# Closing a stage token tile by token tile, with the last rows of the first columns and all rows of the second columns together

## The chip, the cores and the metric

The kernel runs on one core of one Trainium2 chip. The metric is the device time of one execution in microseconds (us); the median of three runs of the kernel before is 2530.16 us.

## The reference

The input is x, 512 tokens by 1024 features, in fp32. It goes through two blocks. The first has two layers: a state-space mixer (S5, with a gated output) and a multi-head latent attention (MLA), each followed by a squared-ReLU feed-forward. The second has two layers of a sparse attention with a spatial gate (DSA), each followed by a gated feed-forward (SwiGLU) with a per-layer embedding p. After each of these eight steps the result is added to the scaled input of the step and normalised:

```python
h = layer_norm(DN_ALPHA * h + mix, ln_mix_g[layer], ln_mix_b[layer])
h = layer_norm(DN_ALPHA * h + sq_relu_mlp(h, w_ff1[layer], w_ff2[layer]), ln_ffn_g[layer], ln_ffn_b[layer])
...
x = layer_norm_2(ALPHA * x + mix, ln1_g[i], ln1_b[i])
...
x = layer_norm_2(ALPHA * x + ffn + ple, ln2_g[i], ln2_b[i])
```

So every step ends with a product of an activation (512 tokens by some rows) with a weight of 1024 columns, the residual sum and a layer norm over the 1024 columns. These eight ends are called closings 1 to 8 here: 1 is the S5 output, 3 MLA, 5 and 7 DSA (`proj_ln`); 2 and 4 are the squared-ReLU feed-forwards, 6 and 8 the SwiGLU ones (`plain`). Closing 8 writes the output.

## The kernel before, in words

**Products.** An fp32 product is three matmuls (`mm3`, L262 to L267): each operand is split into a high and a low part, and high by high, high by low and low by high are summed in PSUM. Rows of a weight are taken in groups of 128, called kts here. A weight arrives by DMA as `wr` (two buffers, four kts of 512 columns in one); `wpiece` (L245) makes pieces of two kts from it: ACT casts the high part `wh`, and VectorE or GpSimd subtracts it to get the low part `wl` (five buffers of each). GpSimd takes the next pieces while the counter `lo_pool` is above zero (L252); it is set to `LP` = 10 at L320, and inside MLA and DSA GpSimd is the engine for all of them.

**A closing.** The 512 tokens are four tiles of 128, the 1024 columns two halves of 512. A pass of eight kts over one tile and one half is 24 matmuls into one PSUM bank. Before the change the first half runs piece by piece over all four tiles, and its four banks are then added to the residual (`update`, L402). The second half has its four pieces ready first and runs tile by tile (`tm_gen` with `stagger`, L323 to L332). After each tile `close` (L422) normalises it on VectorE: residual update from PSUM, statistics (L360, L361), the first pair of full-width operations (L119, one for each half), an inverse square root of 1-element operations (L114, L116, L109), and the second pair (L119). The two x tiles that come out are turned by 8 TensorE transposes (L127) into the feature-major operand of the next stage, cast by ACT (`xh`) and split by VectorE (`xl`). These transposes are queued as pending and are issued one tile at a time: here when more than two are pending (L331), the rest in the next stage's first matmuls (`fm_start`, L462). In MLA and DSA the first half of the closing fills in among the attention's own steps (`proj_first`, L1143).

**Order.** The tile framework's scheduler writes a fixed list of instructions for each engine; on the chip each engine takes its list in order and waits at its head. An instruction that is not ready so holds all behind it on that engine.

Of the kernel before, what the change touches and what calls it, by code (L numbers as in the profile page):

```python
# [8 lines left out]
F32R = mybir.dt.float32r  # L9
# [7 lines left out]
P = 128  # L17
SEQ = 512
NT = SEQ // P
# [28 lines left out]
LP = 10  # L48
# [7 lines left out]
class Cols:  # L56


    def __init__(self, *halves):
        self.halves = halves  # L60
# [6 lines left out]
class Net:  # L67
    def __init__(self, tc, ctx):
        self.tc = tc
        self.nc = tc.nc  # L70
        self.ctx = ctx
        self.n = 0
        self.pending = []
        self.lo_eng = tc.nc.vector
        self.ple = None
        self.lo_pool = 0

    def name(self, tag):
        self.n += 1
        return f"{tag}{self.n}"  # L80
# [161 lines left out]
            self.nc.sync.dma_start(raw[sl] if sl is not None else raw, src)  # L242
        return raw

    def wpiece(self, src):  # L245
        a, b = src.shape[1:]
        hi = self.tile(self.wp, [P, a, b], F32R, "wh", 5)
        lo = self.tile(self.wp, [P, a, b], F32R, "wl", 5)
        self.nc.scalar.copy(hi, src)  # L249
        eng = self.lo_eng  # L250
        if self.lo_pool:
            self.lo_pool -= 1  # L252
            eng = self.nc.gpsimd
        self.tt(lo, src, hi.bitcast(F32), OP.subtract, eng)
        return hi, lo
# [773 lines left out]

    def plain(self, pool, n, H, w, row, gb, final):  # L1030

        gb = self.gb(*gb)
        if final is None:
            self.fm_ln()
        parts = []
        for k in range(2):
            for t in range(2):
                hl = self.tile(pool, [P, 2, n, 256], F32R, "wq", 4)
                self.split(hl[:, 0], hl[:, 1], H[k][t])
                parts.append(hl)  # L1040
        pick = lambda i: (lambda k: Cols(*(parts[k // n * 2 + t][:, i, k % n] for t in range(2))))
        for nh in range(2):
            ev = self.close_ln(gb, nh, False, final) if nh else self.residual(False)(nh)
            self.tm(self.wslab(w, nh * 512, 512, row), list(range(2 * n)), 512, pick(0), pick(1), ev, stagger=nh == 1)

    def strassen(self, pool, n, H, w, row):

# [79 lines left out]
        put(X, 1, 0, OP.add)  # L1127
        yield

    def proj_ln(self, wsrc, xh, xl, gb, order=tuple(range(8)), first=None):  # L1130
        gb = self.gb(*gb)
        if first is None:
            self.new_r()
        self.fm_ln()
        for nh in range(2):
            ev = self.close_ln(gb, nh, True) if nh else self.residual(True)(nh)
            if nh == 0 and first is not None:
                for _ in first:
                    pass
                continue  # L1140
            self.tm(wsrc(nh), list(order), 512, xh, xl, ev, stagger=nh == 1)

    def proj_first(self, wsrc, xh, xl, order=tuple(range(8)), fine=False):  # L1143
        self.new_r()

        def evac(t, ps):
            if self.X is None:
                self.unspill()
            self.residual(True)(0)(t, ps)
        return self.tm_gen(wsrc(0), list(order), 512, xh, xl, evac, fine=fine)  # L1150


    def rope(self, dst, src, half, t, c0):
        nc = self.nc
# [98 lines left out]
    def mla_(self, pool, kv_w_a, kv_norm_g, kv_w_b, q_w_a, q_norm_g, q_w_b, w_o, gb):  # L1253
# [144 lines left out]
        oh, ol = self.fm_x()  # L1398
# [5 lines left out]
            units += [unit(head, qt, shared) for qt in range(NT)]  # L1404
        wsrc = lambda nh: self.wslab(w_o[0], nh * 512, 512)
        pick = lambda x: (lambda k: x[:, k])
        first = self.proj_first(wsrc, pick(oh), pick(ol))
        self.attend(units, 2, [(len(units), first)])
        return lambda: self.proj_ln(wsrc, pick(oh), pick(ol), gb, first=first)


    def sgu_prep(self, sgu_w, sgu_b):
# [42 lines left out]
    def dsa_(self, pool, w_in, w_o, gb, sgu_w, sgu_b, sgu_g, sgu_bt):  # L1455
# [3 lines left out]
        def wsrc(nh):  # L1459
            def src(g):  # L1460
                c = slice(nh * 512, nh * 512 + 512)
                if g[0] >= 4:
                    return [(None, w_o[g[0] * P:(g[-1] + 1) * P, c].rearrange("(k p) m -> p k m", p=P))]
                return [(slice(h * 64, h * 64 + 64), w_o[h * 256:h * 256 + 256, c].rearrange("(k p) m -> p k m", p=64))
                        for h in range(2)]
            return src
# [34 lines left out]
        with self.phase("idx") as sub:  # L1501
# [19 lines left out]
            for t in range(1, NT):  # L1521
                n = (t + 1) * P
                s = score[t]
                qs = slice(t * P, n)
                for h in range(4):
                    bk = self.bank()
                    sl = slice(h % 2 * 64, h % 2 * 64 + 64)
# [21 lines left out]
        with self.phase("sgu") as sub:  # L1549
# [3 lines left out]
            wt, bs, finish = self.sgu_prep(sgu_w, sgu_b)  # L1553
# [95 lines left out]
                        units += [unit(f, g, 2 * half + i, shared) for i in range(2)]  # L1649
            pick = lambda x: (lambda k: A[x][:, k])  # L1650
            order = list(range(4, 8)) + list(range(4))
            first = self.proj_first(wsrc, pick("h"), pick("l"), order, True)

            def some(gen, n):
                for _ in range(n):
# [4 lines left out]
                                     (len(units) + 2, first)])  # L1660


        return lambda: self.proj_ln(wsrc, pick("h"), pick("l"), gb, order, first=first)

    def swiglu(self, p, w_in, w_out, w_ple, w_pg, gb, final):
        ple, self.ple = self.ple, None
# [119 lines left out]
```

## Time and profile before

| what | value |
|---|---|
| median of 3 runs | 2530.16 us (2527.28 to 2530.75) |
| profiled execution: its time, its span | 2529.88 us, 2528.1 us |
| mean granted TensorE clock | 0.973 |
| busy: TensorE matmul, VectorE, ACT, GpSimd | 95%, 62%, 38%, 15% |
| TensorE waits of transposes for a normalised x tile | 30.8 us in 10 waits |
| from TensorE's last matmul to the span's end | 12.8 us |

TensorE is busy nearly all the time, so the shares alone say little: what can be won or lost lies in the few places where its list stands still. A transpose that waits for x (line L127 waiting for VectorE's L119) is such a place, and it stands at each closing.

### The profile page before, as it was taken

What the parts mean: (1) busy time and instruction counts of PE and PEld (TensorE: products, weight loads), DVE (VectorE), ACT (ScalarE), POOL (GpSimd) and SP (SyncE); (2) the same over time, 40 slices, a digit from 0 to 9 for tenths busy, and PEclk for the clock granted to TensorE, in tenths of its full rate; (3) what the DMA queues carried; (4) which work ended last, traced back from release to release, by engine and by line L of the source; (5) the groups of instructions that cost most, each with busy time, mean ns of one, the idle gap of its engine ahead of it and who ended that gap; (6) DMA issues with size and microseconds to landing.
All of it is one profiled execution on the core that took longest, in us unless ns stands there. A gap on an engine that the chain in (4) does not pass through costs nothing.

```text
span 2528.1 us, 30717 instructions
## 1 busy us (share of the span) xinstructions
PE 2411.3 (95%) x11961; PEld 1988.5 (79%) x11961; DVE 1559.1 (62%) x2898; ACT 968.8 (38%) x1563; POOL 389.0 (15%) x378
## 2 busy tenths in 40 slices
PE   7799999999989999999999999999989998999997
PEld 6667888888877888888776878888877687888886
DVE  8744366765666567765695573555569556355655
ACT  4213235445245335444246432333324643223331
POOL 1100110000231220000246220000034622000001
PEclk9779999999999999999999999999999999999999
DMA  4224243322221533222232235232123123423211
GB/s 110 57 57 133 84 150 101 98 88 81 85 71 51 167 92 109 92 92 67 78 127 51 84 121 179 67 133 67 60 86 127 51 86 107 167 67 117 84 59 59
DMA packets 182897, 237.55 MB, mean 94 GB/s; under 512 B 19728, under 2 KB 118816, under 8 KB 182688
## 3 DMA queue, kind: packets, MB, share of 16 engines
q1 hardware_dynamic: 182752, 235.59, 29.5%
q8 instruction: 94, 1.54, 0.3%
q14 instruction: 51, 0.42, 0.1%
HBM read 224.56 MB, written 11.01 MB: 93 GB/s over the span
## 4 chain that ended last, share of the span: by engine, by line
PE 82%; DVE 15%; ACT 2%; DMA 1%; issue 1%; SPq 0%; DVEq 0%; POOL 0%; ACTq 0%
PE ps L265 26%; PE ps L266 25%; PE ps L267 25%; PE ps L127 3%; DVE x L119 2%; PE ps L791 2%; DVE sc L1451 2%; DVE m L1450 2%; DVE x L109 1%; PE ps L789 1%; PE ps L459 1%; DVE vy L109 1%; DVE xl L109 1%; DVE ab L109 1%; DVE sc L119 1%
## 5 line engine op out<-in xcount | busy, mean ns | idle before, releaser
L109 POOL TENSOR_TENSOR wl<-wr,wh 128x1024 fp32r<-128x1024 f32 (+4 forms) x124 | 278.2, 2253 | 1810.9 <-ACT wh L249 1127.0
L249 ACT CAST wh<-wr 128x1024 fp32r<-128x1024 f32 (+4 forms) x300 | 305.7, 1021 | 578.8 <-PE ps L266 287.4
L267 PE MATMUL ps<-xh,wl 128*128 128x512 f32 x1248 | 485.9, 390 | 4.3 <-DVE wl L109 4.3
L265 PE MATMUL ps<-xh,wh 128*128 128x512 f32 x1248 | 486.2, 390 | 0.0
L266 PE MATMUL ps<-xl,wh 128*128 128x512 f32 x1248 | 486.2, 390 | 0.0
L109 DVE TENSOR_TENSOR wl<-wr,wh 128x1024 fp32r<-128x1024 f32 x176 | 217.2, 1236 | 226.5 <-ACT wh L249 225.4
L109 DVE TENSOR_TENSOR wl<-wq,wh 128x1024 fp32r<-128x1024 f32 x140 | 170.5, 1221 | 178.1 <-ACT wh L249 177.7
L267 PEld LDWEIGHTS ps<-xh,wl 128*128 128x128 f32 x1248 | 234.7, 188 | 53.4 <-DVE wl L109 4.7
L265 PE MATMUL ps<-wh,xh 128*128 128x512 f32 (+4 forms) x704 | 270.9, 386 | 4.5 <-DVE rp L109 2.0
L266 PEld LDWEIGHTS ps<-xl,wh 128*128 128x128 f32 x1248 | 234.8, 188 | 48.8
L265 PEld LDWEIGHTS ps<-xh,wh 128*128 128x128 f32 x1248 | 234.6, 188 | 48.6
L266 PE MATMUL ps<-wl,xh 128*128 128x512 f32 (+4 forms) x704 | 263.6, 375 | 0.0
L267 PE MATMUL ps<-wh,xl 128*128 128x512 f32 (+4 forms) x704 | 262.6, 376 | 0.5 <-DVE xl L109 0.5
L249 ACT CAST wh<-wq 128x1024 fp32r<-128x1024 f32 x140 | 147.3, 1052 | 284.1 <-PE ps L266 234.5
L266 PE MATMUL ps<-wl,sh 128*128 128x512 f32 x560 | 217.8, 389 | 0.0
L267 PE MATMUL ps<-wh,sl 128*128 128x512 f32 x560 | 217.5, 389 | 0.0
L265 PE MATMUL ps<-wh,sh 128*128 128x512 f32 x560 | 216.9, 389 | 0.0
L265 PEld LDWEIGHTS ps<-wh,xh 128*128 128x128 f32 x704 | 136.9, 195 | 31.4 <-ACT xh L122 3.5
L267 PEld LDWEIGHTS ps<-wh,xl 128*128 128x128 f32 x704 | 136.1, 194 | 22.1 <-DVE xl L109 1.1
L266 PEld LDWEIGHTS ps<-wl,xh 128*128 128x128 f32 x704 | 137.0, 195 | 18.5
L109 DVE TENSOR_TENSOR x<-x,ps 128x512 f32<-128x512 f32 x156 | 103.0, 681 | 73.4 <-PE ps L267 73.1
L127 PE MATMUL ps<-ident,x 128*128 128x128 f32 x576 | 97.6, 289 | 47.3 <-DVE x L119 30.8
(368 smaller groups left out, 3910.8 us busy)
## 6 DMA issues: line engine op xcount, KB each, us to landing
wr<-in_w_ffn_in_dram SPq DMA_DIRECT2D x44, 1024.0 KB, 5.1
wr<-in_w_ff_dram SPq DMA_DIRECT2D x40, 1024.0 KB, 5.5
wq<-in_w_ff_dram SPq DMA_DIRECT2D x24, 1024.0 KB, 5.1
wq<-in_w_ffn_out_dram SPq DMA_DIRECT2D x16, 1024.0 KB, 8.2
wr<-in_w_in_dram SPq DMA_DIRECT2D x12, 1024.0 KB, 5.5
wr<-in_w_ple_gate_dram SPq DMA_DIRECT2D x8, 1024.0 KB, 5.1
wr<-in_ssm_w_glu_dram SPq DMA_DIRECT2D x6, 1024.0 KB, 5.6
xs<-x SPq DMA_DIRECT2D x24, 256.0 KB, 2.0
```

The lines of the kernel that those rows point to most:

```text
L109: (eng or self.nc.vector).tensor_tensor(out, a, b, op)
L119: (eng or self.nc.vector).scalar_tensor_tensor(out, a, s, b, op0, op1)
L127: self.nc.tensor.transpose(out, in_, self.ident[:k, :k])
L249: self.nc.scalar.copy(hi, src)
L265: mm(ps, lh, rh, start=first, stop=False)
L266: mm(ps, lh, rl, start=False, stop=False)
L267: mm(ps, ll, rh, start=False, stop=last)
L459: self.nc.tensor.matmul(bk[:, c], w[:, kt], self.Xh(kt)[:, c], start=kt == 0 and w is hi, stop=False)
L789: nc.tensor.matmul(o, u[:, q * 8 + j, sl], T[:, m * 2 + h, jj], start=True, stop=False)
L791: nc.tensor.matmul(o, H[sl, r, j], ca[sl, r, j].rearrange("p d c -> p (d c)"), start=False, stop=r == 1)
L1450: self.nc.vector.max(m8, s)
L1451: self.nc.vector.match_replace(s, m8, s, -3e38)
```

## The change

A closing is cut in two functions. `begin` runs the first half of the columns with all but the last four kts, piece by piece over all tiles (in MLA and DSA as the filler among the attention's steps). `finish` has six pieces ready: the two of the last four kts of the first half (`p0`) and the four (three in closing 6, where a stage has six kts) of the second half (`p1`). For each tile it runs `p0`, the update of the first half, `p1` and the close, so a tile has 36 matmuls (30 in closings 6 and 8) where it had 24 (18). The last piece of `p1` lies in additional buffers (`sh`, `sl`). Pending transposes are issued when more than one is pending. `lo_pool` = 10 is set ahead of the six pieces, so four are left for the next stage's pieces where six were. The parameters of the norm and the residual read back from memory are loaded ahead of `finish`.

```diff
@@ -242,10 +243,13 @@
-    def wpiece(self, src):
+    def wpiece(self, src, spare=None):
         a, b = src.shape[1:]
-        hi = self.tile(self.wp, [P, a, b], F32R, "wh", 5)
-        lo = self.tile(self.wp, [P, a, b], F32R, "wl", 5)
+        if spare is None:
+            hi = self.tile(self.wp, [P, a, b], F32R, "wh", 5)
+            lo = self.tile(self.wp, [P, a, b], F32R, "wl", 5)
+        else:
+            hi, lo = (self.tile(spare, [P, a, b], F32R, tag, spare is not self.tail and 2 or 1) for tag in ("sh", "sl"))
...
@@ -1029,9 +1033,6 @@
     def plain(self, pool, n, H, w, row, gb, final):
-        gb = self.gb(*gb)
-        if final is None:
-            self.fm_ln()
...
-        for nh in range(2):
-            ev = self.close_ln(gb, nh, False, final) if nh else self.residual(False)(nh)
-            self.tm(self.wslab(w, nh * 512, 512, row), list(range(2 * n)), 512, pick(0), pick(1), ev, stagger=nh == 1)
+        wsrc = lambda nh: self.wslab(w, nh * 512, 512, row)
+        order, acc = list(range(2 * n)), []
+        for _ in self.begin(wsrc, pick(0), pick(1), order, acc):
+            pass
+        self.finish(wsrc, pick(0), pick(1), order, gb, acc, final, pool)
...
+    def pieces(self, wsrc, kts, spare=None):
+        for i in range(0, len(kts), 4):
+            g = kts[i:i + 4]
+            raw = self.wraw(wsrc(g), len(g), 512)
+            for j in range(0, len(g), 2):
+                m = min(2, len(g) - j)
+                yield self.wpiece(raw[:, j:j + m], spare if i + j + m == len(kts) else None), g[j:j + m]
+
+    def times(self, bank, t, piece, ks, xh, xl, first, last):
...
+    def begin(self, wsrc, xh, xl, order, acc):
+        m = len(order) - 4
+        for pc, ks in self.pieces(wsrc(0), order[:m]):
+            for t in range(NT):
+                if len(acc) <= t:
+                    acc.append(self.bank())
+                self.times(acc[t], t, pc, ks, xh, xl, ks[0] == order[0], False)
+                yield
+
+    def finish(self, wsrc, xh, xl, order, gb, acc, final=None, spare=None):
+        m = len(order) - 4
         gb = self.gb(*gb)
+        if final is None:
+            self.fm_ln()
+        ev0, ev1 = self.residual(False)(0), self.close_ln(gb, 1, False, final)
+        self.lo_pool = LP
+        p0 = list(self.pieces(wsrc(0), order[m:]))
+        p1 = list(self.pieces(wsrc(1), order, spare))
+        for t in range(NT):
+            for pc, ks in p0:
+                self.times(acc[t], t, pc, ks, xh, xl, False, ks[-1] == order[-1])
+            ev0(t, acc[t])
+            bk = self.bank()
+            for pc, ks in p1:
+                self.times(bk, t, pc, ks, xh, xl, ks[0] == order[0], ks[-1] == order[-1])
+            ev1(t, bk)
+            if len(self.pending) > 1:
+                self.flush()
+
+    def proj_ln(self, wsrc, xh, xl, gb, order=tuple(range(8)), first=None, acc=None):
+        order = list(order)
         if first is None:
             self.new_r()
-        self.fm_ln()
-        for nh in range(2):
-            ev = self.close_ln(gb, nh, True) if nh else self.residual(True)(nh)
-            if nh == 0 and first is not None:
-                for _ in first:
-                    pass
-                continue
-            self.tm(wsrc(nh), list(order), 512, xh, xl, ev, stagger=nh == 1)
...
+            acc = []
+            first = self.begin(wsrc, xh, xl, order, acc)
+        for _ in first:
+            pass
+        if self.X is None:
+            self.unspill()
+        with self.phase("tail") as pool:
+            self.tail = pool
+            self.finish(wsrc, xh, xl, order, gb, acc, spare=pool)
+
+    def proj_first(self, wsrc, xh, xl, order=tuple(range(8))):
         self.new_r()
...
+        acc = []
+        return self.begin(wsrc, xh, xl, list(order), acc), acc
```

In closings 1, 2 and 4 TensorE's list follows that order for tiles 0 and 1, then has the first columns of tiles 2 and 3, the transposes of tile 0, the second columns of tile 2, the transposes of tile 1, the second columns of tile 3, and the transposes of tile 2. The place that differs most is closing 5 (the same in 7): the DSA output. TensorE before, from the last matmuls of tile 2's second columns (`ps_12085`); x_11944 and x_11945 are tile 0, `ps_12149` is tile 3's second columns, x_11946 and x_11947 tile 1:

```order
L266 MATMUL ps_12085<-wl_11982,xh_11411 128x512
L267 MATMUL ps_12085<-wh_11981,xl_11412 128x512
L127 MATMUL ps_12135<-ident_68,x_11944 128x128 x4
L127 MATMUL ps_12142<-ident_68,x_11945 128x128 x4
L265 MATMUL ps_12149<-wh_11966,xh_11411 128x512
```

TensorE in the change at the same closing, from the last matmuls of tile 0's (`ps_11957`) and tile 1's (`ps_12020`) second columns; x_11883 and x_11884 are tile 0, `ps_12097` is tile 2's second columns:

```order
L270 MATMUL ps_11957<-sl_11941,xh_11419 128x512
L271 MATMUL ps_11957<-sh_11940,xl_11420 128x512
L270 MATMUL ps_12020<-sl_11941,xh_11419 128x512
L271 MATMUL ps_12020<-sh_11940,xl_11420 128x512
L269 MATMUL ps_12020<-sh_11940,xh_11419 128x512
L270 MATMUL ps_12020<-sl_11941,xh_11419 128x512
L271 MATMUL ps_12020<-sh_11940,xl_11420 128x512
L128 MATMUL ps_12070<-ident_68,x_11883 128x128 x4
L128 MATMUL ps_12077<-ident_68,x_11884 128x128 x4
L269 MATMUL ps_12097<-wh_11925,xh_11419 128x512
```

Tile 0's transposes stood behind tile 2's 24 matmuls; now they stand ahead of them, five matmuls after tile 0's own last one. (Line numbers are one to four higher in the change.)

VectorE in the change at closing 1, from the end of tile 2's inverse square root to its last pair; x_1760 and x_1762 are tile 2, x_1764 and x_1766 tile 3, `ps_2522` is tile 3's second columns, `wl_2842` a piece of the next stage's weights:

```order
L117 TENSOR_SCALAR rq_2481<-rt_2480 128x1
L110 TENSOR_TENSOR wl_2842<-wr_2839,wh_2841 128x1024
L117 TENSOR_SCALAR rq_2481<-rq_2481,rt_2480 128x1
L120 SCALAR_TENSOR_TENSOR x_1766<-x_1766,ps_2522 128x512
L110 TENSOR_TENSOR vy_2477<-vy_2477,rq_2481 128x1
L364 BN_STATS st_2549<-x_1766 128x6
L120 SCALAR_TENSOR_TENSOR x_1760<-x_1760,vy_2477,x_2256 128x512
L120 SCALAR_TENSOR_TENSOR x_1762<-x_1762,vy_2477,x_2258 128x512
```

VectorE before at closing 1, around tile 1's last pair (x_1756 and x_1758), for which the transposes wait there; `ps_2505` is tile 3's second columns:

```order
L109 TENSOR_TENSOR vy_2423<-vy_2423,rq_2427 128x1
L116 TENSOR_SCALAR vy_2473<-rs_2475 128x1
L119 SCALAR_TENSOR_TENSOR x_1756<-x_1756,vy_2423,x_2191 128x512
L119 SCALAR_TENSOR_TENSOR x_1758<-x_1758,vy_2423,x_2193 128x512
L116 TENSOR_SCALAR rt_2476<-vy_2473,ve_2472 128x1
L119 SCALAR_TENSOR_TENSOR x_1766<-x_1766,ps_2505 128x512
```

Before, the pair for which TensorE waits stood ahead of tile 3's update; in the change the pair of tile 2, whose transposes come ahead of the next stage, stands behind tile 3's update, its statistics and a piece of the next stage's weights.

## Rows read from the trace of the kernel before

**Rows 1.** The page: busy us (share of the span) and instructions of each engine.

```profile
PE 2411.3 (95%) x11961; PEld 1988.5 (79%) x11961; DVE 1559.1 (62%) x2898; ACT 968.8 (38%) x1563; POOL 389.0 (15%) x378
```

**Rows 2.** Waits of TensorE: what for, us in total, times, longest.

```profile
PE ps L127 <- DVE x L119: 30.8, 10, 5.5
```

**Rows 3.** Timeline, PE, closings 1 to 7: start, duration, work, [idle before <-releaser].

```profile
333.63 1.97 PE L127 MATMUL ps<-ident,x 128*128 128x128 f32 x8 [5.47 <-DVE x L119]
...
676.42 1.97 PE L127 MATMUL ps<-ident,x 128*128 128x128 f32 x8 [3.15 <-DVE x L119]
...
897.52 1.11 PE L127 MATMUL ps<-ident,x 128*128 128x128 f32 x4 [2.10 <-DVE x L119]
...
1240.35 1.32 PE L127 MATMUL ps<-ident,x 128*128 128x128 f32 x8 [3.21 <-DVE x L119]
...
1470.35 1.77 PE L127 MATMUL ps<-ident,x 128*128 128x128 f32 x8 [4.71 <-DVE x L119]
...
1864.56 1.32 PE L127 MATMUL ps<-ident,x 128*128 128x128 f32 x8 [1.44 <-DVE x L119]
...
1872.34 1.40 PE L127 MATMUL ps<-ident,x 128*128 128x128 f32 x8 [2.35 <-DVE x L119]
...
2101.98 1.85 PE L127 MATMUL ps<-ident,x 128*128 128x128 f32 x8 [4.71 <-DVE x L119]
...
2106.91 1.54 PE L127 MATMUL ps<-ident,a 128*128 128x128 f32 x6 [2.65 <-DMA a<-in_p_dram]
```

**Rows 4.** Timeline, DVE, closing 1: one tile's close with GpSimd idle.

```profile
310.96 0.69 DVE L119 SCALAR_TENSOR_TENSOR x<-x,ps 128x512 f32<-128x512 f32 x1 [4.02 <-PE ps L267]
311.68 0.69 DVE L360 BATCH_NORM_STATS2 st<-x 128x6 f32<-128x512 f32 x1
...
312.73 1.41 DVE L119 SCALAR_TENSOR_TENSOR x<-x,mv,x 128x512 f32<-128x512 f32 x2
...
315.61 0.21 DVE L116 TENSOR_SCALAR rq<-rq,rt 128x1 f32<-128x1 f32 x1
...
317.73 1.40 DVE L119 SCALAR_TENSOR_TENSOR x<-x,vy,x 128x512 f32<-128x512 f32 x2
```

**Rows 5.** Timeline, DVE then POOL, closing 1: the same operations while GpSimd runs.

```profile
324.98 3.56 DVE L119 SCALAR_TENSOR_TENSOR x<-x,mv,x 128x512 f32<-128x512 f32 x2
...
328.52 2.22 DVE L109 TENSOR_TENSOR vy<-vy,rq 128x1 f32<-128x1 f32 x1
...
330.78 3.46 DVE L119 SCALAR_TENSOR_TENSOR x<-x,vy,x 128x512 f32<-128x512 f32 x2
...
325.29 7.74 POOL L109 TENSOR_TENSOR wl<-wr,wh 128x1024 fp32r<-128x1024 f32 x3 [16.21 <-ACT wh L249]
```

**Rows 6.** Timeline, PE, closing 5: matmul pitch, transposes without a wait, matmuls after the wait.

```profile
1458.92 0.39 PE L267 MATMUL ps<-wh,xl 128*128 128x512 f32 x1
1459.15 1.03 PE L127 MATMUL ps<-ident,x 128*128 128x128 f32 x8
...
1472.78 0.63 PE L265 MATMUL ps<-wh,xh 128*128 128x512 f32 x1
```

**Rows 7.** Windows, closing 5 after the wait: length, busy times, granted clock (PEclk), DMA.

```profile
1470.35:1474.00 3.65, 3.65 (x13) 3.02 (x14) 3.65 (x9) 2.40 (x4) 0.23 (x1) 0.54 0.78 270
```

**Rows 8.** The page, costliest groups: low parts of weights, GpSimd and VectorE.

```profile
L109 POOL TENSOR_TENSOR wl<-wr,wh 128x1024 fp32r<-128x1024 f32 (+4 forms) x124 | 278.2, 2253 | 1810.9 <-ACT wh L249 1127.0
...
L109 DVE TENSOR_TENSOR wl<-wr,wh 128x1024 fp32r<-128x1024 f32 x176 | 217.2, 1236 | 226.5 <-ACT wh L249 225.4
```

**Rows 9.** Timeline, DVE, closings 1 and 3: splits of x, and a pair under GpSimd.

```profile
323.36 1.28 DVE L109 TENSOR_TENSOR xl<-ps,xh 128x512 fp32r<-128x512 f32 x2
...
891.92 5.54 DVE L119 SCALAR_TENSOR_TENSOR x<-x,vy,x 128x512 f32<-128x512 f32 x2
```

**Rows 10.** Timeline, closing 8: PE's last matmul, then DVE's last pair.

```profile
2514.92 0.39 PE L267 MATMUL ps<-wh,wq 128*128 128x512 f32 x1
...
2523.67 1.41 DVE L119 SCALAR_TENSOR_TENSOR x<-x,vy,x 128x512 f32<-128x512 f32 x2
```

More of the change, by code (lines that the diff above doesn't have):

```diff
@@ L76, in __init__ @@
         self.lo_pool = 0
+        self.tail = None
     def name(self, tag):
@@ L1128, in strassen @@
         yield
-    def proj_ln(self, wsrc, xh, xl, gb, order=tuple(range(8)), first=None):
-        gb = self.gb(*gb)
+    def pieces(self, wsrc, kts, spare=None):
[6 more added lines that the diff above has]
+    def times(self, bank, t, piece, ks, xh, xl, first, last):
+        hi, lo = piece
+        for i, k in enumerate(ks):
+            self.mm3(bank, xh(k)[:, t * P:(t + 1) * P], xl(k)[:, t * P:(t + 1) * P], hi[:, i], lo[:, i],
+                     first and i == 0, last and i == len(ks) - 1)
@@ L1143, in proj_first @@
-    def proj_first(self, wsrc, xh, xl, order=tuple(range(8)), fine=False):
-        self.new_r()
[L1146 to L1150, printed above, removed]
+            acc = []
[7 more added lines that the diff above has]
+            self.finish(wsrc, xh, xl, order, gb, acc, spare=pool)
@@ L1406, in mla_ @@
         pick = lambda x: (lambda k: x[:, k])
-        first = self.proj_first(wsrc, pick(oh), pick(ol))
+        first, acc = self.proj_first(wsrc, pick(oh), pick(ol))
         self.attend(units, 2, [(len(units), first)])
-        return lambda: self.proj_ln(wsrc, pick(oh), pick(ol), gb, first=first)
+        return lambda: self.proj_ln(wsrc, pick(oh), pick(ol), gb, first=first, acc=acc)
     def sgu_prep(self, sgu_w, sgu_b):
@@ L1651, in dsa_ @@
             order = list(range(4, 8)) + list(range(4))
-            first = self.proj_first(wsrc, pick("h"), pick("l"), order, True)
+            first, acc = self.proj_first(wsrc, pick("h"), pick("l"), order)
             def some(gen, n):
@@ L1660, in dsa_ @@
                                      (len(units) + 2, first)])
-        return lambda: self.proj_ln(wsrc, pick("h"), pick("l"), gb, order, first=first)
+        return lambda: self.proj_ln(wsrc, pick("h"), pick("l"), gb, order, first=first, acc=acc)
     def swiglu(self, p, w_in, w_out, w_ple, w_pg, gb, final):
```

## The prediction

> **What bounds the kernel now.** I read the shares of busy time first: TensorE works 95% of the span, every other engine 62% or less [rows 1]. The change removes and adds no matmul, so what it can win or lose lies in the places where TensorE stands still. The view of waits gives the kind at issue: transposes (L127) waiting for a normalised x, 30.8 us in 10 waits [rows 2]. The timeline of TensorE gives the places [rows 3]: closing 1 5.46 us (the bracket says 5.47), 2 3.15, 3 2.10 (and 0.72 nine us later, in the same timeline), 4 3.21, 5 4.71, 6 1.44 and 2.35, 7 4.71. Their sum, 27.9 us, with the tail of closing 8, is all that the change can win directly.
>
> Why these waits are there is read from VectorE. A tile's close, with GpSimd idle, is: update 0.69, statistics 0.69, first pair 1.41, inverse root until 315.82, second pair 1.40 [rows 4]. From 310.96 to 315.82 that is 4.86, with the last 0.16 us step and the pair 6.4 us. While GpSimd makes low parts, the same pair takes 3.56 and 3.46, and a 1-element product 2.22 [rows 5]; in closing 3 a pair took 5.54 [rows 9]. So an undisturbed close would about fit in the time of the next tile's pass (24 matmuls at 0.23 us, the pitch of neighbouring rows, are 5.5 us, with a set of transposes, 1.03 us [rows 6], 6.5 us), and a disturbed one does not.
>
> **The change part by part.** The change gives each tile 36 matmuls, 8.2 us, and closes should fit in that. Its order, however, does not leave it so.
>
> *Closing 1.* The wait falls on tile 2's transposes. VectorE reaches their last pair only after tile 3's update (0.69), a product (0.15) and statistics (0.69), all of which need the last matmul of tile 3, and 0.7 us of the pair itself: at least 2.2 us. The piece of the next stage's weights in that place is 1.24 us on VectorE [rows 8], and a product and a pair that meet GpSimd cost 2.1 and 2.1 us more [rows 4, 5]: 7.6 us. The nearest row is the same closing now, where both were met, so I take 7.4 against 5.46: +1.9 (from -3.3 to +2.1).
>
> *Closings 2 and 4* have the same order without that piece, and GpSimd's pieces are smaller there. I take no change for each (at least 2.4 us of wait, so -0.8; at most +1.9).
>
> *Closings 5 and 7.* Tile 0's transposes stand five matmuls behind tile 0's last one and directly behind tile 1's, and tile 2's 24 matmuls, ready to run, stand behind them. VectorE's list takes tiles 0 and 1 in turns, step by step. From tile 1's last matmul on it has some 0.3 us left of tile 0's update, tile 1's update 0.66, two statistics 1.3, two aggregates 0.3, two first pairs with their small steps 3.1, sixteen small steps at about 0.13 us 2.0, and half a pair 0.7: 8.4 us of wait (the durations are those of rows 4, with starts about 0.06 apart less). Behind that tile 2's transposes fit if undisturbed, and wait up to 3.3 us if two of GpSimd's pieces meet their last pair; I take 1.5. Next, a piece of weights (1.24) and the update of tile 3 stand ahead of the splits of x (0.64 each [rows 9]) that the next stage's low matmuls need: 0.5 to 1.9, I take 1.8. That is 11.7 against 4.71, +7.0 in closing 5 (from +4.2 to +8.9). In closing 7 the wait for the embedding's DMA, 2.65 us [rows 3], partly passes behind the longer wait: I take +6 (from +1 to +8.9).
>
> *Closing 3* is of the same kind, but 17 matmuls of the first columns and 12 of tile 1 lie between tile 0's last matmul and its transposes (6.6 us). The half of the list that I counted above takes about 12 us from there, because updates of tiles 2 and 3 stand within it too. The wait is 5.4 undisturbed; the pair of 5.54 us is of this closing, so I take 7. With tile 2's transposes (0 to 3.3, taken 1.5) and tile 3's, behind a piece of weights, an update and five splits (3.4), it is 11.9 against 2.8: +9.1 (from +5.6 to +11.9).
>
> *Closing 6.* Tile 2's last pair stands behind tile 3's update, statistics and first pair: 5.2 us at least, with tile 1's transposes about 6.2, against 3.79: +2.4 (from +1 to +4).
>
> *Closing 8.* From the last matmul's end, 2515.31, to the last pair's end, 2525.08, is 9.8 us [rows 10], of which about 3.5 is tiles 1 and 2's own work between. With 30 matmuls per tile that work is done earlier. I take -1.7 (from -3.4 to 0).
>
> *The clock.* After a wait of 4.71 us the granted clock is 0.54 for 3.65 us [rows 7], nearer to 1.2 than to 2.4 GHz: eight transposes take 1.77 instead of 1.03, a matmul 0.63 instead of 0.39 [rows 3, 6]. That costs (1 - 0.54) x 3.65 = 1.7 us. Before, it follows about one wait in each closing; the change has about three more such waits (two in 3, one each in 5 and 7, one fewer in 6): +5.1 (0 to +12).
>
> *What costs nothing.* The matmuls are as many. The six pieces moved ahead (DMAs, casts, low parts) are the ones that were made there anyway; the transfers are hidden behind the attention's or the feed-forward's matmuls, and if that cover were gone each GpSimd piece would cost up to its 2.25 us [rows 8]. The earlier load of the norm's parameters and of the residual lies on SP's queue, which no matmul here waits for.
>
> The sum is 1.9 + 0 + 9.1 + 0 + 7.0 + 2.4 + 6.0 - 1.7 = 24.7, with the clock 29.8. On the profiled execution, 2529.88 us (0.28 under the median, which I leave as noise), it gives 2560 us.
>
> **A rule against the high ends.** In closing 3 the pair that took 5.54 us instead of 1.40 had begun 0.2 us behind a GpSimd piece (891.74 in the timeline); every long pair in these rows is of that kind. The Trainium skill's page "SBUF — State Buffer", section "Who interferes with whom", says of the port pair the two engines share that "Issue order, not op shape, decides who blocks", so a VectorE pair that starts first should go through undisturbed. By that rule, with pairs always first, each term would fall to its lower end, and the sum would be +3.5; no row here shows how often that happens in the new order.
>
> **The rivals.**
>
> *A, faster.* The closes are spaced by the 8.2 us of the new order, and no transpose waits but tile 0's in closings 5 and 7. The waits of 1, 2, 3, 4 and 6 go (18.4 us), 5 and 7 stay about as they are (6.4 - 1.1 against 4.71), closing 8 wins up to 3.4, and five spells of the low clock go (8 us). That is about 25 us less: 2505 us. It decides at tile 2's transposes in closing 1 and tile 0's in closing 3: if they wait under 1 us. For it speaks the 6.4 us close [rows 4]; against it the list of VectorE, in which steps of other tiles stand within a close.
>
> *B, the same.* VectorE's pairs start ahead of GpSimd's pieces, all terms fall to their lower ends, and no clock spells are added: +3.5, 2533 us. For it speaks that four pieces of the next stage, not six, are left to GpSimd; against it that at all seven closings GpSimd now ran first.
>
> *C, slower still.* The six pieces are not ready: `finish` hands six low parts to GpSimd, 6 x 2.25 = 13.5 us one after another, while tile 0 uses them up in 8.2 us. A wait of 5.3 us at each of the seven closings that use GpSimd would come on top: up to +37, about 2595. It decides where the first piece's low part is begun less than 5 us ahead of its first matmul. Against it: GpSimd is busy 15% of the time [rows 1], and the pieces' transfers can begin while the first half runs.
>
> **How the numbers follow.** No change is what a measurement cannot tell from zero, about 0.2% or 5 us: 2525 to 2535. The forecast, slower by 5 to 50 us (the ends of the terms, 2533 to 2580), has 0.58; A 0.20; B 0.10; C 0.12. A's lower part and C's upper part are left out of the range, 2518 to 2580 us. Slower is the forecast and C, 0.70; the same B, 0.10; faster A, 0.20.
>
> **What would show it.** Right: in closings 5 and 7 a wait of 7 to 10 us ahead of tile 0's transposes, in closing 3 one of 5 to 9 us, in closing 1 one of 2 to 8 us at tile 2's, and a sum of waits of transposes for x of about 55 us instead of 30.8. Wrong: waits at these places under 2 us; matmuls of the second columns waiting for `wl` or `sl` (C); or the time lost in the attention's steps, where the filler is halved.

## The result and the profile after

The changed kernel takes 2575.01 us (median of four runs, 2572.97 to 2575.69) where the kernel before took 2530.32 in the same comparison: a ratio of 1.0176, with a 95% interval of 1.0163 to 1.019. The profiled execution spans 2573.6 us, 45.5 more than before; its mean granted clock is 0.962 instead of 0.973. The forecast was 2560.

The page of the kernel after, busy time of each engine (it answers to [rows 1]):

```profile
PE 2430.1 (94%) x11961; PEld 2003.6 (78%) x11961; DVE 1555.6 (60%) x2896; ACT 969.1 (38%) x1563; POOL 396.2 (15%) x380
```

TensorE has the same 11961 matmuls, is busy 18.8 us longer with them (that is the lower clock), and stands still for the other 26.7 us of the 45.5.

The view of TensorE's waits, kernel after (what for, us in total, times, longest; against [rows 2]):

```profile
PE ps L128 <- DVE x L120: 55.0, 13, 7.8
...
PE ps L128 <- ACT x L1534: 8.8, 2, 7.5
...
PE ps L128 <- DMA a<-in_p_dram: 5.3, 1, 5.3
```

The first row was forecast as "about 55 us". The second belongs to the attentions' steps, and no term of the sum has it: before, the same kind of wait was 3.7 us, 2.4 in the first DSA attention and 1.3 in the second, where it is 7.5 now.

The timeline of TensorE, kernel after, the waits at closings 1 to 7 (start, duration, work, [idle before <-releaser]; they answer to [rows 3]), with one row, at 1951.32, from the second DSA attention:

```profile
335.17 1.97 PE L128 MATMUL ps<-ident,x 128*128 128x128 f32 x8 [5.58 <-DVE x L120]
...
678.68 1.97 PE L128 MATMUL ps<-ident,x 128*128 128x128 f32 x8 [4.12 <-DVE x L120]
...
889.15 1.94 PE L128 MATMUL ps<-ident,x 128*128 128x128 f32 x8 [6.32 <-DVE x L120]
...
906.86 1.78 PE L128 MATMUL ps<-ident,x 128*128 128x128 f32 x8 [2.67 <-DVE x L120]
...
917.82 1.94 PE L128 MATMUL ps<-ident,x 128*128 128x128 f32 x8 [2.47 <-DVE x L120]
...
1252.91 1.97 PE L128 MATMUL ps<-ident,x 128*128 128x128 f32 x8 [3.37 <-DVE x L120]
...
1476.11 1.94 PE L128 MATMUL ps<-ident,x 128*128 128x128 f32 x8 [7.83 <-DVE x L120]
...
1493.87 1.78 PE L128 MATMUL ps<-ident,x 128*128 128x128 f32 x8 [2.65 <-DVE x L120]
...
1898.08 1.97 PE L128 MATMUL ps<-ident,x 128*128 128x128 f32 x8 [5.73 <-DVE x L120]
...
1951.32 0.69 PE L128 MATMUL ps<-ident,x 128*128 128x128 f32 x2 [7.53 <-ACT x L1534]
...
2131.56 1.94 PE L128 MATMUL ps<-ident,x 128*128 128x128 f32 x8 [7.83 <-DVE x L120]
...
2149.24 1.78 PE L128 MATMUL ps<-ident,x 128*128 128x128 f32 x8 [2.67 <-DVE x L120]
...
2156.74 1.51 PE L128 MATMUL ps<-ident,a 128*128 128x128 f32 x6 [5.30 <-DMA a<-in_p_dram]
```

Closings 3, 5 and 7 have a long wait at tile 0's transposes and one of 2.7 us at tile 2's (closing 3 one more, at tile 3's); closings 1, 2, 4 and 6 have one each. In closing 7 the embedding's DMA is waited for behind that, longer than before.

**Why tile 0 waits 7.83 us.** The timeline of VectorE at closing 5, kernel after; TensorE's last matmul ahead of the wait, tile 1's, starts at 1467.89:

```profile
1465.37 1.28 DVE L120 SCALAR_TENSOR_TENSOR x<-x,ps 128x512 f32<-128x512 f32 x2 [3.73 <-PE ps L271]
1466.57 1.28 DVE L364 BATCH_NORM_STATS2 st<-x 128x6 f32<-128x512 f32 x2
1467.77 1.27 DVE L120 SCALAR_TENSOR_TENSOR x<-x,ps 128x512 f32<-128x512 f32 x2
1468.95 1.28 DVE L364 BATCH_NORM_STATS2 st<-x 128x6 f32<-128x512 f32 x2
...
1470.44 1.40 DVE L120 SCALAR_TENSOR_TENSOR x<-x,mv,x 128x512 f32<-128x512 f32 x2
...
1471.89 1.40 DVE L120 SCALAR_TENSOR_TENSOR x<-x,mv,x 128x512 f32<-128x512 f32 x2
...
1475.21 2.74 DVE L120 SCALAR_TENSOR_TENSOR x<-x,vy,x 128x512 f32<-128x512 f32 x4
```

Two tiles are closed together, step by step: two updates, two statistics, two first pairs, then sixteen small steps two by two, and both second pairs in one row. GpSimd has no piece after 1469.11, and nothing here is drawn out (a pair takes 1.40 as in [rows 4]); the list alone is that long. Why both tiles end together is seen on GpSimd and ACT. The timeline of GpSimd, then of ACT, kernel after:

```profile
1462.34 2.40 POOL L110 TENSOR_TENSOR sl<-wr,sh 128x1024 fp32r<-128x1024 f32 x1 [10.94 <-ACT sh L253]
```

```profile
1460.81 0.37 ACT L123 CAST xh<-ps 64x256 fp32r<-64x256 f32 x1 [6.58 <-PE ps L271]
1461.20 1.05 ACT L253 CAST sh<-wr 128x1024 fp32r<-128x1024 f32 x1
```

`sl`, the low part of the last piece of the second columns, is begun only here and ends at 1464.74, 3.2 us ahead of tile 1's last matmul: its cast `sh` stands on ACT right behind a cast of the attention's, because the additional buffers are opened after the attention's steps. So both tiles' last matmuls, five or six each, are all that is left to run when it lands. Run e5 takes this piece away.

**Where the rest went.** To place the loss, the start of the same matmul, counted along TensorE's list, was read in both traces at the bounds of each stage; the table gives the growth of each stage's length against the kernel before, in us (noise about 2.5: in e8, where nothing differs from the kernel before up to closing 6, closing 2 reads -2.0 and DSA1 2.4). Closings are c1 to c8; "other" is the S5 mixer and the four feed-forwards together; "sum" is the span.

```
kernel          c1    c2   c3    c4   c5    c6    c7   c8  | MLA  DSA1  DSA2 | other   sum
after           0.4  -0.5 11.5  -0.1  8.9   1.4   8.7 -2.0 | 0.3   1.9  13.7 |  1.3   45.5
e1_flush2      -3.0  -6.1  1.8  -6.0  7.4  -4.4  12.6 -2.0 |-0.4   0.0  11.7 |  1.7   13.2
e2_lp6         -1.3  -0.6 13.7  -0.9 14.4   0.5  11.5 -2.0 | 0.4   1.8   5.2 | -1.2   41.4
e3_proj_only    0.3  -2.1  9.7   0.0  8.3  -1.7   8.9 -0.3 |-0.5  -0.2   2.8 |  2.1   27.3
e4_plain_only   0.0  -0.7  0.0  -1.0  0.0   1.1  -0.3 -1.6 | 0.4   4.5  13.1 | -0.6   14.9
e5_late2        4.8   0.5  9.6   0.3  5.9   0.6   4.5 -1.4 | 6.8   0.7  12.4 | -2.4   42.5
e6_plain_s5    -3.0  -6.2  0.3  -6.1  0.7  -4.8  -0.2 -2.5 |-0.3   6.4  10.5 |  2.1   -2.9
e7_268         -0.1  -6.2  0.1  -0.1 -0.1  -4.8  -0.5 -2.5 |-0.2  -0.4  12.6 |  1.8   -0.5
e8_68           0.0  -2.0  0.0   0.3 -0.1  -4.4   0.1 -2.0 |-0.6   2.4   0.9 |  1.0   -4.4
e9_best_lp6    -1.1  -6.0  0.0  -6.0 -0.2  -4.3  -0.2 -2.0 | 0.9   2.5   1.1 | -0.2  -15.6
e10_best_lp4   -0.9  -6.0  0.0  -5.9 -0.1  -4.1   0.0 -1.7 | 0.5   2.5   4.1 |  1.0  -10.6
```

In the changed kernel the closings lose 28.3 us and the three attentions 15.9, of which 13.7 are in the second DSA. That last number is made of waits and clock. ACT's timeline, kernel after, at the wait of 7.53 us:

```profile
1946.94 0.27 ACT L123 CAST a<-ps 128x128 fp32r<-128x128 f32 x1 [9.70 <-DVE rp L110]
```

and before, at the same place (the line moved by one):

```profile
1916.49 0.27 ACT L122 CAST a<-ps 128x128 fp32r<-128x128 f32 x1 [3.98 <-DVE rp L109]
```

ACT waits for two small rope products on VectorE. In VectorE's list 46 steps of the top-k search (L1495, L1496, 0.36 us on average) of this attention stand ahead of the first of them, where 31 stood before: then it started 5.1 us after the first of ACT's four copies of that stage (1911.12 to 1916.19), now 11.5 us (1935.13 to 1946.64). TensorE's waits in this attention sum to 16.6 us instead of 10.2. The rest is the clock. Windows of the kernel after (length, busy time of PE, PEld, DVE, ACT, POOL with counts, granted clock, DMA share, GB/s), behind the wait of 7.53 us, behind one of 2.19 at 2014.73 and one of 1.89 at 2033.50:

```profile
1951.30:1955.00 3.70, 3.68 (x10) 2.99 (x11) 3.70 (x17) 1.76 (x5) 1.78 (x2) 0.50 0.00 0
...
2016.70:2023.40 6.70, 6.70 (x21) 5.22 (x22) 2.46 (x8) 3.32 (x10) 6.70 (x11) 0.50 0.01 2
2033.80:2043.90 10.10, 10.10 (x30) 7.70 (x30) 2.15 (x11) 4.40 (x11) 4.45 (x7) 0.50 0.15 33
```

and of the kernel before in the same attention, behind waits of 2.08 and 2.96 us:

```profile
1897.34:1900.74 3.40, 3.40 (x22) 3.08 (x20) 2.37 (x7) 3.38 (x9) 1.07 (x1) 0.50 0.89 338
1975.85:1979.26 3.41, 3.41 (x10) 2.53 (x9) 3.09 (x20) 1.50 (x7) 1.28 (x4) 0.50 0.00 0
```

Length times (1 - clock) sums to 10.3 us after and 3.4 before. So 6.4 us of waits and 6.9 of clock stand against the 13.7 measured.

### The profile page after: what moved, and what is told of

Its sections match the earlier page's. It is cut to its first block, busy times and chain, and to the rows that moved or that the text cites. A ratio compares the mean times of both kernels' runs of the same rounds, so it can differ in the third digit from the quotient of the medians.

```text
span 2573.6 us, 30731 instructions
## 1 busy us (share of the span) xinstructions
PE 2430.1 (94%) x11961; PEld 2003.6 (78%) x11961; DVE 1555.6 (60%) x2896; ACT 969.1 (38%) x1563; POOL 396.2 (15%) x380
## 4 chain that ended last, share of the span: by engine, by line
PE 81%; DVE 14%; issue 2%; ACT 2%; DMA 1%; POOL 0%; SPq 0%; DVEq 0%; ACTq 0%; POOLq 0%
PE ps L269 25%; PE ps L270 24%; PE ps L271 24%; PE ps L128 3%; DVE x L120 2%; PE ps L795 2%; DVE sc L1496 2%; DVE m L1495 1%; DVE x L110 1%; PE ps L463 1%; PE ps L793 1%; DVE st L364 1%; DVE xl L110 1%; DVE vy L110 1%; PE ps L696 1%
## 5 line engine op out<-in xcount | busy, mean ns | idle before, releaser
L110 POOL TENSOR_TENSOR wl<-wr,wh 128x1024 fp32r<-128x1024 f32 (+4 forms) x118 | 265.9, 2264 | 1800.3 <-ACT wh L253 1797.1
L253 ACT CAST wh<-wr 128x1024 fp32r<-128x1024 f32 (+4 forms) x292 | 297.2, 1020 | 637.1 <-PE ps L271 300.9
L269 PE MATMUL ps<-wh,xh 128*128 128x512 f32 (+4 forms) x680 | 265.5, 391 | 2.2 <-DVE rp L110 1.6
L270 PE MATMUL ps<-wl,xh 128*128 128x512 f32 (+4 forms) x680 | 257.2, 378 | 0.0
L271 PE MATMUL ps<-wh,xl 128*128 128x512 f32 (+4 forms) x680 | 255.5, 377 | 0.0
L128 PE MATMUL ps<-ident,x 128*128 128x128 f32 x576 | 103.3, 303 | 75.5 <-DVE x L120 55.0
L128 PEld LDWEIGHTS ps<-ident,x 128*128 128x128 f32 x576 | 75.1, 154 | 102.8 <-DVE x L120 36.4
```

The lines of the kernel that those rows point to most:

```text
L110: (eng or self.nc.vector).tensor_tensor(out, a, b, op)
L128: self.nc.tensor.transpose(out, in_, self.ident[:k, :k])
L269: mm(ps, lh, rh, start=first, stop=False)
L270: mm(ps, lh, rl, start=False, stop=False)
L271: mm(ps, ll, rh, start=False, stop=last)
```

## The experiments

All are edits of the changed kernel, and all compute the whole result. The ratios are against the kernel before, run beside it on the same chip.

**e1_flush2: transposes one tile later.** The changed kernel issues pending transposes when more than one is pending, the kernel before when more than two are.

```diff
-            if len(self.pending) > 1:
+            if len(self.pending) > 2:
                 self.flush()
```

> Edit: transposes are issued when more than two are pending, as before the change; all else as changed. The list of TensorE then has tile 0's transposes of closings 3, 5 and 7 behind tile 2's 24 matmuls. Theory T (the loss at these closings is the wait of transposes that stand ahead of ready matmuls): the waits for tile 0 there, 6.3, 7.8 and 7.8 us in the changed kernel, fall under 1 us, what waits later in the same closing stays under 5 us, and closings 3, 5 and 7 together lose 10 us or less against the kernel before instead of 30. Rival P (the loss is GpSimd's pieces that hold VectorE up, whatever the order): the waits only move to other tiles and these closings still lose 25 us or more. The steps of the two DSA attentions stand in another order than in both kernels, so that the total is only bounded: by T 2535 to 2560 us, by P 2565 or more.

Measured: 2542.94 us, 1.0047 (1.0032 to 1.0062). Its view of waits:

```profile
PE ps L128 <- DVE x L120: 29.2, 7, 9.7
```

26 of the 55 us go, and most of closing 3's loss with them (1.8 left of 11.5). But closings 3, 5 and 7 still lose 21.8 us together, more than theory T allows (10) and less than rival P asks for (25): T holds in closing 3 and fails in 5 and 7. Closings 1, 2, 4 and 6 now gain 3 to 6 us each, which I had not expected: with 36 matmuls per tile and one more tile's distance most of their closes fit. Closings 5 and 7 get longer waits instead, and in closing 7 one wait for the embedding's DMA takes 8.61 us. TensorE's, then VectorE's timeline of e1_flush2 at closing 5:

```profile
1457.10 1.94 PE L128 MATMUL ps<-ident,x 128*128 128x128 f32 x8 [9.73 <-DVE x L120]
```

```profile
1446.71 1.41 DVE L120 SCALAR_TENSOR_TENSOR x<-x,mv,x 128x512 f32<-128x512 f32 x2
...
1450.08 2.01 DVE L120 SCALAR_TENSOR_TENSOR x<-x,mv,x 128x512 f32<-128x512 f32 x2
...
1453.04 1.40 DVE L120 SCALAR_TENSOR_TENSOR x<-x,mv,x 128x512 f32<-128x512 f32 x2
...
1456.22 1.40 DVE L120 SCALAR_TENSOR_TENSOR x<-x,vy,x 128x512 f32<-128x512 f32 x2
```

There the place of the transposes alone does not make the wait; with either threshold VectorE has several tiles' closes in front of it at once, here three first pairs ahead of the first second pair. And the second attention still loses 11.7.

**e2_lp6: fewer low parts on GpSimd.** `lo_pool` leaves none for the next stage's pieces, so VectorE makes them.

```diff
-        self.lo_pool = LP
+        self.lo_pool = 6
```

> Edit: the counter of pieces for GpSimd is set to 6 instead of 10 ahead of a closing's six pieces, so that the next stage's first pieces go to VectorE and none of GpSimd's falls into a close (inside MLA and DSA the first stage behind it too). Theory P (GpSimd's pieces in the closes are a large part of the loss): the waits for tile 2's transposes, 5.6, 4.1, 2.7, 3.4, 2.7, 5.7 and 2.7 us in closings 1 to 7 of the changed kernel, fall by 2 us or more each, together by 15 us. Theory T: the waits for tile 0 in closings 3, 5 and 7 (6.3, 7.8, 7.8 us) stay within 0.7 us, because no piece falls into them, and the others fall by 1 to 2 us each (the floor of 2.2 us in closing 1 stays, and each piece costs VectorE 1.24 us). Total by P alone 2560, by T 2565 to 2572, without what the attention's own order does.

Measured: 2575.72 us, 1.0179 (1.0162 to 1.0196), as the changed kernel; but that hides two changes, since the closings lose 35.3 us instead of 28.3 and the second attention 5.2 instead of 13.7. Both theories expected shorter waits behind the closes; the waits grow:

```profile
PE ps L128 <- DVE x L120: 69.2, 13, 9.0
```

The timeline of VectorE in e2_lp6 between the first and second pair of closing 3's tile 2 shows why:

```profile
898.26 1.23 DVE L110 TENSOR_TENSOR wl<-wr,wh 128x1024 fp32r<-128x1024 f32 x1
899.41 0.15 DVE L117 TENSOR_SCALAR vy<-rs 128x1 int32<-128x1 int32 x1
899.68 1.22 DVE L110 TENSOR_TENSOR wl<-wr,wh 128x1024 fp32r<-128x1024 f32 x1
900.82 0.27 DVE L117 TENSOR_SCALAR rt<-vy,ve 128x1 f32<-128x1 f32 x1
901.03 1.23 DVE L110 TENSOR_TENSOR wl<-wr,wh 128x1024 fp32r<-128x1024 f32 x1
```

Three pieces of weights, 3.7 us, have moved into the middle of a close, and tile 3's update and four splits of x come behind them; the transposes there wait 7.72 us instead of 2.67. In the changed kernel the same place is disturbed by GpSimd, in VectorE's and GpSimd's timelines:

```profile
901.84 1.86 DVE L110 TENSOR_TENSOR vy<-vy,rt 128x1 f32<-128x1 f32 x1
...
904.48 1.53 DVE L110 TENSOR_TENSOR vy<-vy,rq 128x1 f32<-128x1 f32 x1
```

```profile
901.28 4.71 POOL L110 TENSOR_TENSOR wl<-wr,wh 128x1024 fp32r<-128x1024 f32 x2 [13.08 <-ACT wh L253]
```

Two 1-element products that take 0.16 elsewhere take 1.86 and 1.53 when they begin behind a GpSimd piece. The Trainium skill's page "SBUF — State Buffer", section "Who interferes with whom", says that issue order decides who blocks whom; the trace agrees, both begin after a piece has. That costs some 3 us here, less than the three pieces on VectorE. So handing these pieces to VectorE does not win the loss back, and the longest waits, 7.83 us in closings 5 and 7, have no such product in them. What the closings would lose with the pieces on neither engine was not tried.

**e3_proj_only and e4_plain_only: half of the closings each.** e3 has the new form in closings 1, 3, 5 and 7 (with the attentions' filler half as long), e4 in 2, 4, 6 and 8 (with the filler as before). In e3 `plain` is the function before, in e4 `proj_ln` and `proj_first` are the functions before. The end of e3's edit:

```diff
...
-        self.finish(wsrc, pick(0), pick(1), order, gb, acc, final, pool)
+        for nh in range(2):
+            ev = self.close_ln(gb, nh, False, final) if nh else self.residual(False)(nh)
+            self.tm(self.wslab(w, nh * 512, 512, row), list(range(2 * n)), 512, pick(0), pick(1), ev, stagger=nh == 1)
```

> Edit: only closings 1, 3, 5 and 7 (the projections) have the new form, 2, 4, 6 and 8 the old one. In the changed kernel the two DSA attentions themselves lose about 17 us (3 and 14), outside any closing. Theory L (their VectorE steps were listed in another order because closings 2, 4 and 6 end otherwise; here the list of these steps is that of the kernel before): the attentions stand within 2 us of before, closings 1, 3, 5, 7 lose 0.4 + 12 + 9 + 9, total about 2560 us. Rival F (the attentions lose because only half of the first columns' product is left to fill their waits): they still lose 14 us or more, total about 2577 us.

> Edit: only closings 2, 4, 6 and 8 have the new form; the projections 1, 3, 5, 7 and their filler are as before. Theory L (the order in which the DSA attentions are listed costs the 17 us; here it is that of the changed kernel): these attentions lose 14 to 18 us, closings 2, 4, 6 and 8 together -2 to +1, total about 2545 us. Rival F (the halved filler costs it): nothing is lost in the attentions, total 2528 to 2531 us.

Measured: e3 2560.1 us, 1.0117 (1.0098 to 1.0136); e4 2545.42 us, 1.0058 (1.0043 to 1.0073). The table shows two separate losses. e3 has the loss of closings 3, 5 and 7 (26.9 of its 27.3) and only 2.8 in the second attention, although the filler is halved there. e4 leaves those closings as they were, changes its own by -2.2 in sum, and loses 4.5 and 13.1 in the two DSA attentions, none of whose code it touches. The waits in e4:

```profile
PE ps L128 <- ACT x L1538: 8.8, 2, 7.5
```

That is the row of the changed kernel again; e3 has 2.7 with 1.6 the longest. So the loss in the attention comes with the closings of the feed-forwards ahead of it, not with the halved filler. What is left is the order that the scheduler writes; why it lists the top-k steps earlier when the stage ahead is changed was not followed.

**e5_late2: two kts late instead of four, and no additional memory.** In closings 1, 3, 5 and 7 `finish` has five pieces, one of the first half and four of the second, all in the `wh` and `wl` buffers, so none has to wait for the attention's memory.

```diff
-        m = len(order) - 4
+        m = len(order) - late
...
-        with self.phase("tail") as pool:
-            self.tail = pool
-            self.finish(wsrc, xh, xl, order, gb, acc, spare=pool)
+        self.finish(wsrc, xh, xl, order, gb, acc, late=2)
```

> Edit: in the projections (closings 1, 3, 5, 7) only the last two kts of the first columns, not four, run in the new form, so that five pieces suffice, and no piece lies in additional memory; the closings 2, 4, 6, 8 as changed, and the attentions' steps are listed as in the changed kernel. Theory S (in closings 5 and 7 the last piece of the second columns is made only when the attention has let its memory go, so that tiles 0 and 1 end within 1.1 us of each other and VectorE closes both at once, which makes the 7.8 us waits): without that piece tile 0 ends 30 matmuls ahead of its transposes, and the waits for tile 0 in closings 5 and 7 fall from 7.8 us to under 2; closings 5 and 7 lose at most 3 us instead of 9; total about 2562 us. Rival I (VectorE's list interleaves the tiles' closes anyway): those waits stay at 5 us or more and the total at 2570 or more.

Measured: 2569.19 us, 1.0161 (1.0146 to 1.0176). TensorE's timeline of e5_late2 at closing 5:

```profile
1478.11 1.84 PE L128 MATMUL ps<-ident,x 128*128 128x128 f32 x8 [4.11 <-DVE x L120]
```

7.83 became 4.11, neither under 2 (theory S) nor over 5 (rival I): about half of that wait went with the late last piece. The edit also takes a tile from 36 to 30 matmuls and gives two kts back to `begin`, so that the piece alone is not separated. In the 4.11 us other tiles' updates still stand inside tile 0's close, and its last pair, begun at 1475.98 behind a GpSimd piece of 1475.17, takes 2.74 us instead of 1.40. Whether a list that finishes tile 0 first would remove them was not tried. Tile 2's wait grew to 4.69, closing 1 loses 4.8 and MLA 6.8, so little is won.

**e6 to e8: only where it wins.** With the later flush, the new form only in closings 1, 2, 4, 6, 8 (e6), in 2, 6, 8 (e7) and in 6, 8 (e8); the others, and the attentions' filler, are as before. In `plain` (a counter marks the closing):

```diff
     def plain(self, pool, n, H, w, row, gb, final):
+        self.nplain = getattr(self, "nplain", 0) + 2
+        if self.nplain in (2, 4, 6, 8):
+            return self.plain_new(pool, n, H, w, row, gb, final)
```

> Edit: transposes issued when more than two are pending, and the new form only in closings 1, 2, 4, 6 and 8; 3, 5 and 7 with their filler are as before. Theory B (with tile 0's transposes behind tile 2's matmuls the new form wins where no attention ends; e1 showed -2.9, -5.6, -5.3 and -5.3 us in closings 1, 2, 4 and 6, and the changed kernel -1.8 at the end): closings together -19 to -21 us, closings 3, 5 and 7 within 1 us of before. The attentions are listed in a new order, which cost nothing to 15 us in the kernels so far: total 2509 to 2526 us, faster than before. Rival M (the wins of e1 are won time that the next stage gives back): closings together -5 or less, total 2525 us or more.

> Edit: as e6, but the new form only in closings 2, 6 and 8. The first DSA attention is listed as in the kernel before. Theory B: -5.6, -5.3 and -1.8 us in closings 2, 6 and 8, the first DSA attention within 2 us of before, total 2517 us if the second attention's new order costs nothing and 2532 us if it costs 15. Rival M: 2525 to 2540 us.

> Edit: as e6, but the new form only in closings 6 and 8. Nothing differs from the kernel before up to closing 6. Theory B: -5.3 and -1.8 us, total 2523 us, plus what the second DSA attention's new order costs (0 to 15 us). Rival M: 2528 to 2545 us.

Measured: e6 2527.22 us, 0.9993 (0.9983 to 1.0002); e7 2531.67, 1.0006 (0.9996 to 1.0015); e8 2524.88, 0.9981 (0.9971 to 0.9991). In e6 the changed closings gain 22.6 us in sum, more than theory B said, and the attentions lose 16.6, more than the 15 it allowed, so hardly anything is left and the total misses its range. Rival M let the closings themselves gain little; they gain 22.6, 13.5 and 6.4 us in e6, e7 and e8, and e8's total lies below M's range, while those of e6 and e7 alone would fit M. TensorE's timeline of e6, in the second attention:

```profile
1918.58 0.66 PE L128 MATMUL ps<-ident,x 128*128 128x128 f32 x2 [10.47 <-DVE a L110]
```

The same attention with the same code now waits at another operation. In e7 it loses 12.6, in e8, without closing 2, 0.9. So its loss takes the values 0.9, 2.8, 10.5, 12.6, 13.1 and 13.7 with edits that are all outside its own steps but for e3's and the changed kernel's filler.

**e9_best_lp6 and e10_best_lp4: e6 with another `lo_pool`.** The value was varied because it changes VectorE's and GpSimd's shares, and so the list, near the attention.

```diff
-        self.lo_pool = LP
+        self.lo_pool = 6
```

> Edit: e6 (transposes when more than two are pending, the new form in closings 1, 2, 4, 6 and 8 alone) with the counter for GpSimd at 6 instead of 10. The one number changes how the scheduler lists the attentions: the first DSA attention's VectorE steps stand as in e1, the second's as in e8, where they cost 0.0 and +0.9 us, while those of e6 cost 6.4 and 10.5. Theory L (the order of the list decides what the attentions lose): closings 1, 2, 4, 6 and 8 win 20 to 22 us as in e6, the attentions lose 2 us or less, total 2507 to 2513 us. Rival (the attentions give back what the closings win, whatever their order): total 2522 us or more, as e6.

> Edit: as e9 with the counter at 4, so that two of a closing's six pieces go to VectorE as well; the attentions are listed as in e9. Theory L: the attentions as in e9; each closing has 2 x 1.24 us more on VectorE ahead of its closes, which are done by then: within 4 us of e9, total 2507 to 2516 us. Rival: 2522 us or more.

Measured: e9 2514.25 us, 0.9937 (0.9924 to 0.995); e10, with 4, 2515.62, 0.994 (0.9927 to 0.9954), not to be told from it. e9 stands 1.2 us above theory L's range, since the attentions lose 4.5 us and not 2; the rival's 2522 us is ruled out. The waits in e9:

```profile
PE ps L128 <- DVE x L120: 20.1, 7, 4.7
```

The plain closings keep their gain (18.3 us in 2, 4, 6 and 8), and the second attention loses 1.1. TensorE's own list in that attention tells the runs apart as well: in the traces of e8, e9 and e10 its operations follow each other as in the kernel before, in those of e2 and e3 nearly so (losses of 0.9 to 5.2 us), and in the changed kernel, e1, e4, e5, e6 and e7 they are ordered differently (10.5 to 13.7 us). So what is shown is that the loss goes with the scheduler's order; how much of it is VectorE's list and how much TensorE's no run separates. This version beats both kernels: 0.6% under the one before, and by the ratios 0.9937 / 1.0176 = 0.9765 about 2.3% under the changed one.

## Why the prediction was right, and which term was mis-sized

**Direction and mechanism** were as forecast: VectorE's list, in which steps of other tiles stand inside a close, lets transposes wait that the change puts closer behind their tiles. e1 shows the second half of it: with the transposes one tile later, closing 3 loses 1.8 us instead of 11.5.

**Closings.** The terms with the clock summed to +29.8, measured +28.3; that the sum is this close is in part luck, since misses of up to 1.5 us in single closings partly cancel, and the noise of each is larger. Closing 3: 9.1 and two spells of 1.7 at the low clock make 12.5, measured 11.5, with waits of 6.32, 2.67 and 2.47 for 7, 1.5 and 3.4. Closing 5: 7.0 and one spell make 8.7, measured 8.9; the wait is 7.83 for 8.4, tile 2's 2.65 for 1.5. Closing 6: 2.4 less one spell is 0.7, measured 1.4 (wait 5.73 for 6.2). Closings 2 and 4, taken at 0, gave -0.5 and -0.1. Closing 8, -1.7, measured -2.0: from the last matmul's end to the last pair's it is 7.97 us instead of 9.77. TensorE's, then VectorE's timeline at the end, kernel after ([rows 10] before):

```profile
2562.24 0.39 PE L271 MATMUL ps<-sh,wq 128*128 128x512 f32 x1
```

```profile
2569.19 1.41 DVE L120 SCALAR_TENSOR_TENSOR x<-x,vy,x 128x512 f32<-128x512 f32 x2
```

**Small misses among them.** Closing 1 was taken at a wait of 7.4, since both operations that met GpSimd before were expected to meet it again; this time the last product and pair took 0.15 and 1.40, and an earlier product (1.50) and the piece of weights on VectorE (2.94 instead of 1.24) met it; the wait was 5.58 and the term 0.4 instead of 1.9. Closing 7: the DMA's wait of 2.65 us was to pass partly behind the longer wait; it grew to 5.30, because SyncE issues this load at 2151.43, behind tile 2's transposes, and so behind all the waits for x (before, at 2101.87, as the wait of 4.71 ended). The term is 8.7 for 6 and one spell, 7.7. A low spell was priced at 1.7 us from [rows 7]; behind the longer wait in closing 5 it lasts 4.89 us at 0.53, so (1 - 0.53) x 4.89 = 2.3. The ends of closing 3's term, +5.6 and +11.9, do not follow from the parts shown, which give +6.0 and +10.9; the forecast does not hang on them. The window of the kernel after, closing 5:

```profile
1476.11:1481.00 4.89, 4.89 (x16) 4.22 (x17) 1.84 (x3) 0.00 (x0) 0.00 (x0) 0.53 0.01 3
```

**The term that was mis-sized** is "What costs nothing": the attentions and their filler have no term in the sum and so stood at 0, without a reason given; they measured 15.9 us, which is nearly the whole distance from 2560 to 2575. The text named "the time lost in the attention's steps, where the filler is halved" as what would prove it wrong, and that sign came true beside the right ones. The place was right, the reason was not: e4 shows the loss with the filler as before, e3 hardly any with the filler halved. The step that failed is so the one that took the attentions, whose own steps are not edited, to run as before; their lists had changed. The diff of the changed kernel's lists was read at the closings alone; the rope products on VectorE in the second attention would have stood in it.

**The rivals.** A's deciding point, waits under 1 us at closing 1's tile 2 and closing 3's tile 0, failed (5.58 and 6.32). But its idea, that closes fit the spacing of 36 matmuls, holds in closings 1, 2, 4 and 6 (there 30) once the transposes come one tile later (e1, e6): the order was what spoilt it, not the pace. B failed: the closings lose 28.3 us, not 3.5, operations still begin behind GpSimd's pieces, and the longest waits have none of these in them. The issue order on which B rests also decides for each operation and not for a pair. The prediction took every long pair to have begun behind a piece, but the one of 3.56 us in [rows 5] begins at 324.98, ahead of the piece at 325.29; VectorE's timeline of the kernel before, one operation at a time:

```profile
324.98 0.75 DVE L119 SCALAR_TENSOR_TENSOR x<-x,mv,x 128x512 f32<-128x512 f32 x1
...
325.64 2.90 DVE L119 SCALAR_TENSOR_TENSOR x<-x,mv,x 128x512 f32<-128x512 f32 x1
```

The first operation goes ahead of the piece undisturbed, the second, behind it, is held up.

C, low parts that come too late for their matmuls, did not show as a wait for `wl` or `sl` at a closing; yet a low part that came late went with two tiles' ending together in closing 5 (e5).

## What to carry to other kernels

Spacing work out for one engine helped here only where the operation that waits for it was moved back as well: closings 1, 2, 4 and 6 differ by 3 to 6 us each by the threshold of one `if`, closing 3 by 9.7; 5 and 7 were not helped. Where a scheduler writes the lists, compare them in stages that the edit does not touch, too, above all on the engine with a long list of small steps; here an attention that no edit touched lost between 0.9 and 13.1 us (e8, e4), and 6 us of its waits in the changed kernel stand behind two products of 0.17 us. And time each half of a change by itself: closings that gain and closings that lose were hidden in one sum.

## What was not expected of the hardware

Short waits can be followed by more loss than their own: behind waits of 2.19 and 1.89 us in the second attention the granted clock was 0.50, 1.2 of 2.4 GHz, for 6.7 and 10.1 us (the windows above), so 4.1 us of waiting had 8.4 us of lost clock behind it. Behind waits of 2.08 and 2.96 us in the same attention before, it was 0.50 for 3.4 us each, so the length of the wait alone does not give the price. And a product of one element per partition is drawn out to 1.5 to 1.9 us behind a GpSimd piece of 2.4, as a pair of full-width operations is.
